# The samples' query attention of a hybrid decoder step: cache loads for two samples at a time, both heads in 1 KB pieces

## The chip, the cores and the metric

One Trainium2 chip; the kernel runs on one of its cores. The time is the device time of one execution in microseconds (us), here the median of three runs. Names used below: TensorE (PE in rows, PEld for its weight loads), VectorE (DVE), ScalarE (ACT), GpSimd (POOL), SyncE (SP). SP computes nothing; it issues the kernel's DMAs in a fixed order, one queue for all of them. DMAs run on 16 DMA engines of the core.

## What is computed

One inference step of a two-layer decoder, for a prompt of 4096 tokens and, beside it, for 8 samples of one new token each. Layer 0 is a dilated sliding-window attention, layer 1 a grouped-query attention over a window of 128 with a learned sink per head: 16 query heads share 2 key-value heads of 64 elements. The change touches layer 1 for the samples only. Cut to that:

```python
def swa_sink_sample(q, kv_ext, n_past, sinks):     # kv_ext: 128 cached rows and the new one
    B, S, HQ, hd = q.shape
    HKV = kv_ext.shape[3]; G = HQ // HKV
    qg = q.reshape(B, S, HKV, G, hd)
    s = jnp.einsum('bskgd,bjkd->bkgsj', qg, kv_ext[:, :, 0]) * hd ** -0.5
...
    p, den = sink_softmax(s, mask, sink)
    o = jnp.einsum('bkgsj,bjkd->bskgd', p, kv_ext[:, :, 1]) / jnp.moveaxis(den, -1, 1)[..., None]
    return o.reshape(B, S, HQ * hd)
```

The cache `cache_b_kv` is laid out as (8 samples, 128 positions, key or value, 2 heads, 64 elements) in float32, so the keys and values of both heads at one position are 256 elements, 1 KB, in one piece of memory, and one head's keys at one position are 256 B.

## The kernel before

The program is unrolled by a Python generator and nothing reorders it afterwards: each engine runs its instructions in the order in which they were written. The prompt is worked in seven passes over 32 tiles of 128 tokens: three passes `a`, then `c`, two passes `b` (pass 4 for key-value head 0, pass 5 for head 1), then `d`. A tile has 48 ticks. In each tick one projection matmul is issued (line 650, `ps_pj<-wt,xT`), and tables (`PB0`, `PB1` for the b passes) say at which tick, counted from the tile's start, the tile's other steps are issued; steps reach into the next two tiles. Of a b tile the steps that matter here are, with the ticks of pass 4 and of pass 5:

- `turn`, -64 and -39: a DMA transpose brings the tile's activations, `xT<-x1s` (L174).
- `load`, -12 and -3: SP loads `tab` (L927), in pass 5 also `KV<-kvd` (L930).
- `kvs`, 37, pass 4 only: SP stores the keys and values of the tile, `kvd<-KV` (L968).
- `tp0` to `tp3`, 93, 94, 100, 103 and 84, 88, 96, 103: four DMA transposes of probabilities, `PT<-PS` (L598), one for each pair of heads. VectorE makes PS.
- `va0` to `va3`, 110, 112, 126, 131 and 96, 109, 124, 127: TensorE multiplies PT by the values, `ps_o<-KV,PT` (through the helper at L97).
- `sum0`, `sum1`: VectorE divides into `uo` (L1033), of which there is one buffer; then `ubd<-uo` (L1050) stores it on SP.

At the end of a tile one copy of a cache to its output goes to SP too (L1596, `out_a_s<-in_cache_a_kv_g`).

The samples' work is a side program, a generator of small steps. `PACE` holds a number for each pass; every `PACE` ticks, in tiles 1 to 29, one step of the side program is taken ("a pump"), and its instructions land between the tiles' own on each engine. `wait()` is four empty steps. In pass 4 the side program runs `samples_kv`, `samples_b(0)` and then the split of pass 5's weights (`weights_pass`, loads at L314); in pass 5 it runs `samples_b(1)` and then pass 6's weights, which begin with a burst of four loads `st<-in_w_o_b`.

`samples_b` (L1312) is what changes. It takes the eight samples in two rounds of four. In each round SP issues four DMAs: for keys, then for values, a load of 127 cached positions (L1334, `s_half<-in_cache_b_kv`), one position to a partition, and a small copy of the new token's row into partition 127 (L1336, `s_half<-kvsd`). Five pumps later TensorE turns the keys (L1341, `ps_kTs`), and scores, softmax and values follow step by step. `s_half` is a pool of four buffers of 128 x 512 float32.

Of the kernel before, what the change touches and what calls it, by code (L numbers as in the profile page):

```python
# [9 lines left out]
F32 = mybir.dt.float32  # L10
# [5 lines left out]
ALU = mybir.AluOpType  # L16
# [36 lines left out]
PD = dict(load=-100, stat=-75, rstd=-67, high=-60, low=-57, turn=-31, loadx=10, gp=42, sq0=47, sq1=57, rstd2=76,  # L53
          add=77, store=85)

PACE = [3.66, 5.6, 5.15, 9, 8.8, 9, 16]
GAP = [0, 0, 0, 0, 0, 0, 0]


# [5 lines left out]
def decoder_kernel(ctx: ExitStack, tc: tile.TileContext, I, O):  # L65
    nc = tc.nc
    dma = nc.sync.dma_start
# [18 lines left out]
    sp = ctx.enter_context(tc.tile_pool(name="samp", bufs=1))  # L86
# [4 lines left out]
    sx_ps = ctx.enter_context(tc.tile_pool(name="sx", bufs=1, space=PSUM))  # L91
# [4 lines left out]
    def mm(out, lhsT, rhs, start, stop):  # L96
        nc.tensor.matmul(out, lhsT, rhs, start=start, stop=stop)  # L97
# [4 lines left out]
    ident = cpool.tile([128, 128], F32, name="ident")  # L102
# [31 lines left out]
    kvsd = dr.tile([NS, 256], F32, name="kvsd")  # L134
# [45 lines left out]
    def s_half():  # L180
        return sp.tile([128, 512], F32, name="s_half", tag="s_half", bufs=4)

    def load_s(src):
        t = s_half()
        n, w = src.shape
        dma(t[:n, :w], src)
        return t[:n, :w]
# [349 lines left out]
    def gate(t, z):  # L537

        nc.scalar.activation(t, z, AF.Tanh, scale=0.5)
        gate2(t, z)  # L540
# [568 lines left out]
    def wait():  # L1109
        for _ in range(WAIT):  # L1110
            yield
# [68 lines left out]
    def s_rope(src, heads):  # L1180

        t1 = sp.tile([128, 512], F32, name="s_rope", tag="s_rope")[:NS]
        t2 = s_half()
        rope_mult(src, rope_s, t1, t2, NS, heads)
        return t1
# [126 lines left out]
    def samples_b(jh, q, z):  # L1312
        snk = sp.tile([NS, 1], F32, name="snk", tag="snk")
        dma(snk, I["sinks_b"][0, jh * 8:(jh + 1) * 8].unsqueeze(1))
        R = s_rope(q[:NS], 8)
        sz = sp.tile([128, 512], F32, name="gate_s", tag="gate_s")
        gate(sz[:NS], z[:NS])
        yield
        yield
        ps = sx_ps.tile([64, 8, NS], F32, name="ps_qTs", tag="sx")  # L1320
        for h in range(8):
            nc.tensor.transpose(ps[:, h, :], R[:, h * 64:(h + 1) * 64], ident[:NS, :NS])
        yield
        QTs = sp.tile([64, NS, 8], F32, name="QTs", tag="QTs")
        nc.vector.tensor_copy(QTs.rearrange("p b h -> p h b"), ps)
        m = sp.tile([8, NS], F32, name="m_s", tag="m_s")
        l = sp.tile([8, NS], F32, name="l_s", tag="l_s")
        on = s_half()
        src = I["cache_b_kv"].rearrange("b j s h e -> j b s h e")
        for q4 in range(2):  # L1330
            bs = slice(4 * q4, 4 * q4 + 4)
            kvt = s_half().rearrange("p (b s e) -> p b s e", b=4, s=2)
            for s in range(2):
                dma(kvt[0:127, :, s, :], src[1:128, bs, s, jh, :])  # L1334
                o = s * 128 + jh * 64
                dma(kvt[127:128, :, s, :], kvsd[bs, o:o + 64].unsqueeze(0))  # L1336
            yield from wait()
            yield
            pk = sx_ps.tile([64, 4, 128], F32, name="ps_kTs", tag="sx")
            for k in range(4):  # L1340
                nc.tensor.transpose(pk[:, k, :], kvt[:, k, 0, :], ident)  # L1341
            yield
            KTs = s_half().rearrange("p (b e) -> p b e", b=4)
            nc.scalar.copy(KTs[:64], pk)
            yield
            yield
            sc = sx_ps.tile([8, 4, 128], F32, name="ps_scs", tag="sx")
            for k in range(4):
                mm(sc[:, k, :], QTs[:, 4 * q4 + k, :], KTs[:64, k, :], True, True)
            yield  # L1350
            nc.vector.tensor_reduce(out=m[:, bs], in_=sc, axis=AX.X, op=ALU.max)
            nc.vector.tensor_scalar(m[:, bs], m[:, bs], SCALE, snk, op0=ALU.mult, op1=ALU.max)
            nc.vector.tensor_scalar(m[:, bs], m[:, bs], -1.0, None, op0=ALU.mult)
            yield
            P = s_half()
            for k in range(4):
                b = 4 * q4 + k
                nc.scalar.activation(P[:8, k * 128:(k + 1) * 128], sc[:, k, :], AF.Exp, bias=m[:, b:b + 1], scale=SCALE,
                                     accum_out=l[:, b:b + 1])
            yield  # L1360
            yield
            ps = sx_ps.tile([128, 4, 8], F32, name="ps_sPb", tag="sx")
            for k in range(4):
                nc.tensor.transpose(ps[:, k, :], P[:8, k * 128:(k + 1) * 128], ident[:8, :8])
            yield
            PTs = sp.tile([128, 4, 8], F32, name="PTsb", tag="PTs")
            nc.vector.tensor_copy(PTs, ps)
            yield
            po = sx_ps.tile([8, 4, 64], F32, name="ps_sob", tag="sx")
            for k in range(4):  # L1370
                mm(po[:, k, :], PTs[:, k, :], kvt[:, k, 1, :], True, True)
            yield
            es = sp.tile([8, 4], F32, name="es_s", tag="es_s")
            nc.vector.tensor_scalar(es, m[:, bs], snk, None, op0=ALU.add)
            nc.scalar.activation(es, es, AF.Exp)
            nc.vector.tensor_tensor(l[:, bs], l[:, bs], es, op=ALU.add)
            nc.vector.reciprocal(l[:, bs], l[:, bs])
            nc.vector.scalar_tensor_tensor(on[:8, q4 * 256:(q4 + 1) * 256].rearrange("p (b e) -> p b e", e=64), po, 0.5,
                                           l[:, bs].unsqueeze(2).to_broadcast([8, 4, 64]), op0=ALU.mult, op1=ALU.mult)
            yield  # L1380
        dma(usd[jh].rearrange("b (h e) -> h b e", e=64), on[:8].rearrange("p (b e) -> p b e", e=64))
        yield from wait()
        o2 = load_s(usd[jh])
        yield from wait()
        nc.vector.tensor_tensor(o2, o2, sz[:NS], op=ALU.mult)
        yield
        dma(ubd_s[:, HV[jh]], o2)
# [147 lines left out]
    def pump(gen, n=1):  # L1535
        for _ in range(n):
            if next(gen, True) is True:
                return

    def side(pi):  # L1540

        if pi < 3:
            if pi == 0:
                yield from s_start()
                samp[0] = yield from weights_pass(0, None, [samp["hS0"]] * 2, False)
            if pi == 2:
                mix_factors()
            yield from samples_a(order[pi][1], *samp[pi])
            yield from ada_units([(v, i) for v in VEC[2 + 2 * pi:4 + 2 * pi] for i in range(2)])
            if pi < 2:  # L1550
                samp[pi + 1] = yield from weights_pass(pi + 1, [G0c] * 2, [samp["hS0"]] * 2)
            else:
                yield from samples_c(3)
        elif pi == 3:
            Gk, G1 = load_cols("Gkv"), load_cols("G1")
            yield from wait()
            samp[4] = yield from weights_pass(4, [Gk, G1, G1], [samp["hSk"], samp["hS1"], samp["hS1"]])
        elif pi == 4:
            yield from samples_kv(samp[4][0])
            yield from samples_b(0, *samp[4][1:])  # L1560
            G1 = load_cols("G1")
            yield from wait()
            samp[5] = yield from weights_pass(5, [G1] * 2, [samp["hS1"]] * 2)
        elif pi == 5:
            yield from samples_b(1, *samp[5])
            yield from samples_d(6)
# [14 lines left out]
    for tick in range(min(at), max(at) + 1):  # L1581
# [6 lines left out]
        pi, it, s = tiles[n][0], n % NB, tick - start[n]  # L1588
        if it == 1 and s == 0:
            begun = tick  # L1590
        if 1 <= it < NB - 2 and (tick - begun) % PACE[pi] >= PACE[pi] - 1:
            pump(sides[pi])
        if n + 1 < N and tick + 1 == start[n + 1]:
            if copies and n >= 2 and order[pi][0] != "c":
                o, i = copies.pop(0)
# [59 lines left out]
```

## Time and profile before

| | us |
|---|---|
| median of 3 runs | 3038.01 |
| lowest and highest run | 3031.45, 3038.73 |
| the profiled execution, its whole time | 3039.8 |
| its span from first to last instruction | 3037.9 |

| engine | busy us | share of the span |
|---|---|---|
| PE | 2898.5 | 95% |
| DVE | 1885.8 | 62% |
| ACT | 1859.2 | 61% |
| POOL | 798.3 | 26% |

Shares are means over seven passes. What a change in the two b passes is worth is read there: pass 4 begins near 1620 us, pass 5 near 2180 us of the span. In the lists of waits a line reads: engine, tile and line that waited, what it waited for, us in total, times, the longest. The chain of work that ended last is followed backwards from the end of the kernel; an engine's name with a q (SPq) is time in which its queue was held by an instruction.

### The profile page before, as it was taken

What the parts mean: (1) busy time and instruction counts of PE and PEld (TensorE: products, weight loads), DVE (VectorE), ACT (ScalarE), POOL (GpSimd) and SP (SyncE); (2) the same over time, 40 slices, a digit from 0 to 9 for tenths busy, and PEclk for the clock granted to TensorE, in tenths of its full rate; (3) what the DMA queues carried; (4) which work ended last, traced back from release to release, by engine and by line L of the source; (5) the groups of instructions that cost most, each with busy time, mean ns of one, the idle gap of its engine ahead of it and who ended that gap; (6) DMA issues with size and microseconds to landing.
All of it is one profiled execution on the core that took longest, in us unless ns stands there. A gap on an engine that the chain in (4) does not pass through costs nothing.

```text
span 3037.9 us, 57543 instructions
## 1 busy us (share of the span) xinstructions
PE 2898.5 (95%) x20600; PEld 1486.8 (49%) x20600; DVE 1885.8 (62%) x4797; ACT 1859.2 (61%) x4606; POOL 798.3 (26%) x989
## 2 busy tenths in 40 slices
PE   7999989999999999998998899999979999999998
PEld 2444434544445444444444566666545555544444
DVE  4655565545556677875665567776756677764443
ACT  4766676555666667766554567666656777763332
POOL 0422111211112333343332223233322222331121
PEclk8999999999999999999999899999999999999999
DMA  7898996787857799779996569777657988798975
GB/s 240 207 250 231 281 260 157 163 184 186 192 128 168 190 235 224 170 174 313 287 257 172 116 136 204 157 147 138 137 115 151 199 190 169 156 223 231 218 200 159
DMA packets 1092888, 585.97 MB, mean 193 GB/s; under 512 B 925156, under 2 KB 1003509, under 8 KB 1089896
## 3 DMA queue, kind: packets, MB, share of 16 engines
q1 hardware_dynamic: 1092600, 582.29, 80.3%
q8 instruction: 161, 2.64, 0.4%
q14 instruction: 127, 1.04, 0.1%
HBM read 243.76 MB, written 159.26 MB: 133 GB/s over the span
## 4 chain that ended last, share of the span: by engine, by line
PE 73%; DMA 8%; DVE 6%; ACT 4%; SPq 4%; issue 3%; POOL 1%; DVEq 0%; POOLq 0%; ACTq 0%
PE ps_pj L650 50%; PE ps_sc L650 7%; PE ps_o L97 4%; DMA PT<-PS 4%; PE ps_sc L97 3%; PE ps_kv L97 3%; SPq L1336 2%; PE ps_sc L562 2%; PE ps_tr L616 1%; PE ps_s L210 1%; PE ps_tr L1000 1%; DMA st<-in_w_in_a_dram 1%; ACT P L584 1%; DMA xT<-usdp 1%; PE ps_ada L210 1%
## 5 line engine op out<-in xcount | busy, mean ns | idle before, releaser
L650 PE MATMUL ps_pj<-wt,xT 128*128 128x512 f16 x9024 | 2180.7, 382 | 33.8 <-ACT ps_pj L631 23.6
L650 PEld LDWEIGHTS <-xT 128*128 128x128 f16 x10368 | 965.4, 98 | 1054.0 <-issue 113.7
L535 POOL TENSOR_TENSOR rope<-rope,rope 128x512 f32<-128x512 f32 x160 | 264.2, 1651 | 899.7 <-DVE rope L530 866.5
L593 DVE SCALAR_TENSOR_TENSOR PS<-P,PS 128x512 f16<-128x512 f32 (+1 forms) x448 | 300.6, 691 | 167.0 <-ACT PS L592 165.9
L530 DVE SCALAR_TENSOR_TENSOR rope<-ps_pj,scl,tab 128x512 f32<-128x512 f32 x320 | 225.0, 744 | 149.7 <-PE ps_pj L650 149.2
L584 ACT ACTIVATE P<-P,nm_b 128x256 f32<-128x256 f32 (+1 forms) x512 | 252.9, 494 | 103.6 <-DVE nm_b L577 102.9
L631 ACT ACTIVATE ps_pj<-bias,scl 128x512 f32<-128x512 f32 x318 | 219.2, 689 | 146.4 <-DVE rope L530 71.1
L650 PE MATMUL ps_sc<-wt,xT 128*128 128x512 f16 x1344 | 297.0, 379 | 0.7 <-DMA xT<-usdp 0.7
L97 PEld LDWEIGHTS <-PT 128*128 128x128 f16 x5076 | 207.3, 98 | 177.6 <-DMA PT<-PS 81.3
L592 ACT ACTIVATE PS<-P 128x512 f16<-128x512 f32 (+1 forms) x448 | 258.0, 597 | 54.9 <-DMA PT<-PS 51.4
L577 DVE CUSTOM_DVE_ANT_0 P<-ps_sc,masks,nsink 128x256 f32<-128x256 f32 (+1 forms) x512 | 249.4, 534 | 4.0 <-PE ps_sc L97 3.9
L577 DVE CUSTOM_DVE_ANT_0 P<-ps_sc,masks,scl 128x256 f32<-128x256 f32 (+1 forms) x384 | 154.4, 450 | 128.0 <-PE ps_sc L562 94.9
L97 PE MATMUL ps_o<-KV,PT 128*128 128x64 f16 x3024 | 131.7, 194 | 46.4 <-DMA PT<-PS 46.4
L97 PE MATMUL ps_sc<-KTb,QTb 128*128 128x256 f16 (+1 forms) x1024 | 153.3, 273 | 10.5 <-ACT QTb L1004 5.3
L584 ACT ACTIVATE P<-P,U 128x256 f32<-128x256 f32 (+1 forms) x256 | 118.3, 463 | 65.1 <-DVE U L577 62.2
L863 DVE TENSOR_TENSOR ss<-ss 128x1 f32<-128x1 f32 x64 | 10.2, 159 | 206.8 <-ACT junk L858 206.5
L97 PEld LDWEIGHTS <-QTb 128*128 128x128 f16 x1024 | 99.2, 98 | 76.0 <-ACT QTb L1004 12.5
L142 POOL TENSOR_SCALAR rm_t<-ss 128x1 f32<-128x1 f32 (+2 forms) x132 | 26.9, 203 | 392.2 <-ACT xs L158 336.2
L1004 ACT COPY QTb<-ps_tr 128x1024 f16<-128x1024 f16 x64 | 64.8, 1012 | 90.4 <-PE ps_tr L1000 90.2
L867 POOL TENSOR_TENSOR rs<-rm_t,mhalf 128x1 f32<-128x1 f32 x64 | 38.9, 607 | 279.2 <-DVE rm_t L866 278.7
L858 ACT ACTIVATE junk<-ps_sc 128x512 bf16<-128x512 f32 x64 | 38.1, 595 | 119.2 <-PE ps_sc L650 114.4
L1045 POOL TENSOR_TENSOR uo<-uo,gate 128x512 f32<-128x512 f32 x64 | 93.1, 1455 | 53.1 <-DVE uo L1033 17.8
(256 smaller groups left out, 3519.6 us busy)
## 6 DMA issues: line engine op xcount, KB each, us to landing
out_a_s_dram<-in_cache_a_kv_g_dram SPq DMA_DIRECT2D x144, 256.0 KB
x_t<-in_x_prompt_dram SPq DMA_DIRECT2D x64, 512.0 KB
st<-in_w_in_a_dram SPq DMA_DIRECT2D x96, 256.0 KB
xsd<-xs SPq DMA_DIRECT2D x32, 512.0 KB
st<-in_ada_w_dram SPq DMA_DIRECT2D x32, 512.0 KB
x1d<-x_t SPq DMA_DIRECT2D x32, 512.0 KB
st<-in_w_in_b_dram SPq DMA_DIRECT2D x32, 512.0 KB
x1s<-xs SPq DMA_DIRECT2D x32, 512.0 KB
```

The lines of the kernel that those rows point to most:

```text
L97: nc.tensor.matmul(out, lhsT, rhs, start=start, stop=stop)
L210: nc.tensor.matmul(ps[q:q + QR, :w.shape[-1]], hS[:, c, :], w, start=c < 4, stop=c + 4 >= nch, tile_position=(0, q))
L530: nc.vector.scalar_tensor_tensor(t[:n, :w].rearrange("p (h e) -> p h e", e=64), s3, scale, tab[:n, o:o + 64].unsqueeze(1).to_broadcast([n, ...
L535: nc.gpsimd.tensor_tensor(a4, a4, b4[:, :, ::-1, :], op=ALU.add)
L577: nc.vector.tensor_tensor_reduce(out=self.P[:, j, :n], in0=self.sc[j][:, :n], in1=self.mask[:, :n], scale=self.nss, scalar=self.init[j], o ...
L584: nc.scalar.activation(self.P[:, j, :n], self.P[:, j, :n], AF.Exp, bias=self.nm[j], scale=-1.0, accum_out=self.l[j])
L592: nc.scalar.activation(S[:, 0], P, AF.Copy, scale=PSC)
L593: nc.vector.scalar_tensor_tensor(S[:, 1], P, PSC, S[:, 0], op0=ALU.mult, op1=ALU.subtract)
L631: nc.scalar.activation(t[f"ps{hf}"], bias[pi, hf], AF.Copy, scale=scl[pi][:, IDS:IDS + 1])
L650: nc.tensor.matmul(t[f"ps{hf}"], t[hT][:, p, c, :], ws()[hf][c][q], start=c == 0 and k == 0 and not biased, stop=c == n - 1 and k == 2, sk ...
L1004: nc.scalar.copy(t["QT"], t["tq"])
L1045: nc.gpsimd.tensor_tensor(t["uo"], t["uo"], t["sz"], op=ALU.mult)
```

## The change

`samples_b` takes four rounds of two samples in place of two rounds of four. A round has one load in place of two: it brings, for two samples, keys and values of both heads, though the call uses one head (`jh`), in pieces of 256 elements (1 KB) in place of 64 (256 B). The buffer keeps its size, 512 elements a partition. The row of the new token is one copy of 512 elements a round in place of two copies of 4 x 64. All steps behind the loads are the same with two samples in place of four, so a call has 32 steps more; `PACE` of passes 4 and 5 goes from 8.8 and 9 to 7.3 ticks.

```diff
-PACE = [3.66, 5.6, 5.15, 9, 8.8, 9, 16]
+PACE = [3.66, 5.6, 5.15, 9, 7.3, 7.3, 16]
...
-        src = I["cache_b_kv"].rearrange("b j s h e -> j b s h e")
-        for q4 in range(2):
-            bs = slice(4 * q4, 4 * q4 + 4)
-            kvt = s_half().rearrange("p (b s e) -> p b s e", b=4, s=2)
-            for s in range(2):
-                dma(kvt[0:127, :, s, :], src[1:128, bs, s, jh, :])
-                o = s * 128 + jh * 64
-                dma(kvt[127:128, :, s, :], kvsd[bs, o:o + 64].unsqueeze(0))
+        src = I["cache_b_kv"].rearrange("b j s h e -> j b (s h e)")
+        for q in range(4):
+            bs = slice(2 * q, 2 * q + 2)
+            kvt = s_half().rearrange("p (b s e) -> p b s e", b=2, e=64)
+            k4 = kvt.rearrange("p b s e -> p b (s e)")
+            dma(k4[0:127], src[1:128, bs])
+            dma(k4[127:128], kvsd[bs].unsqueeze(0))
             yield from wait()
             yield
-            pk = sx_ps.tile([64, 4, 128], F32, name="ps_kTs", tag="sx")
-            for k in range(4):
-                nc.tensor.transpose(pk[:, k, :], kvt[:, k, 0, :], ident)
+            pk = sx_ps.tile([64, 2, 128], F32, name="ps_kTs", tag="sx")
+            for k in range(2):
+                nc.tensor.transpose(pk[:, k, :], kvt[:, k, jh, :], ident)
...
-            for k in range(4):
-                mm(po[:, k, :], PTs[:, k, :], kvt[:, k, 1, :], True, True)
+            for k in range(2):
+                mm(po[:, k, :], PTs[:, k, :], kvt[:, k, 2 + jh, :], True, True)
...
```

How this moves SP's queue is seen at three places. In the rows, 127x4x64 is 127 partitions of four pieces of 64 elements; "x2" stands for two such rows in succession; the changed file is one line shorter, so that L1336 becomes L1335 and L1596 becomes L1595.

SP in pass 4 before, the second round:

```order
L598 DMA_TRANSPOSE PT<-PS 128x8x128 x2
L1596 DMA out_a_s_dram<-in_cache_a_kv_g_dram 16x4096
L1334 DMA s_half<-in_cache_b_kv_dram 127x4x64
L1336 DMA s_half<-kvsd 1x4x64
L1334 DMA s_half<-in_cache_b_kv_dram 127x4x64
L1336 DMA s_half<-kvsd 1x4x64
L1050 DMA ubd_2_276<-uo 128x512
L598 DMA_TRANSPOSE PT<-PS 128x8x128 x2
```

The same pass now, the second round (the fourth stands in the same way) and then the third:

```order
L598 DMA_TRANSPOSE PT<-PS 128x8x128 x2
L1334 DMA s_half<-in_cache_b_kv_dram 127x2x256
L1335 DMA s_half<-kvsd 1x512
L174 DMA_TRANSPOSE xT<-x1s_183 128x16x128
L927 DMA tab<-in_rope_dram 128x128
L968 DMA kvd_245<-KV 128x320
L598 DMA_TRANSPOSE PT<-PS 128x8x128 x2
```

```order
L968 DMA kvd_247<-KV 128x320
L1334 DMA s_half<-in_cache_b_kv_dram 127x2x256
L1335 DMA s_half<-kvsd 1x512
L598 DMA_TRANSPOSE PT<-PS 128x8x128 x2
L1595 DMA out_a_s_dram<-in_cache_a_kv_g_dram 16x4096
L1050 DMA ubd_4_278<-uo 128x512
```

The double load between the two pairs of PT has become single loads that stand, in rounds 2 and 4, between a tile's last PT and the next xT, and in rounds 1 and 3 between the kvd store and the first PT.

SP in pass 5, where the first and the third round stand as the two old rounds did (xT, load, copy, PT); the second and the fourth now:

```order
L598 DMA_TRANSPOSE PT<-PS 128x8x128
L1334 DMA s_half<-in_cache_b_kv_dram 127x2x256
L1335 DMA s_half<-kvsd 1x512
L598 DMA_TRANSPOSE PT<-PS 128x8x128
L174 DMA_TRANSPOSE xT<-x1s_182 128x16x128
```

```order
L598 DMA_TRANSPOSE PT<-PS 128x8x128 x2
L1334 DMA s_half<-in_cache_b_kv_dram 127x2x256
L1335 DMA s_half<-kvsd 1x512
L927 DMA tab<-in_rope_dram 128x128
L930 DMA KV<-kvd_250 128x320
L1050 DMA ubd_6_312<-uo 128x512
L1595 DMA out_a_s_dram<-in_cache_a_kv_g_dram 16x4096
L598 DMA_TRANSPOSE PT<-PS 128x8x128 x2
```

Round 2 has moved between a tile's third and fourth PT, round 4 between its second and third, ahead of four other DMAs.

## Rows read from the trace of the kernel before

**Rows 1.** The page: the chain that ended last, its lines.

```profile
PE ps_pj L650 50%; PE ps_sc L650 7%; PE ps_o L97 4%; DMA PT<-PS 4%; PE ps_sc L97 3%; PE ps_kv L97 3%; SPq L1336 2%; PE ps_sc L562 2%; PE ps_tr L616 1%; PE ps_s L210 1%; PE ps_tr L1000 1%; DMA st<-in_w_in_a_dram 1%; ACT P L584 1%; DMA xT<-usdp 1%; PE ps_ada L210 1%
```

**Rows 2.** PE's timeline: start, us, line, op, tiles, count, [idle before <-releaser].

```profile
1672.35 0.50 PE L97 MATMUL ps_o<-KV,PT 128*128 128x64 f16 x6 [9.02 <-DMA PT<-PS]
...
1736.38 0.82 PE L97 MATMUL ps_o<-KV,PT 128*128 128x64 f16 x12 [10.58 <-DMA PT<-PS]
...
2228.03 0.50 PE L97 MATMUL ps_o<-KV,PT 128*128 128x64 f16 x6 [10.79 <-DMA PT<-PS]
...
2283.11 0.82 PE L97 MATMUL ps_o<-KV,PT 128*128 128x64 f16 x12 [9.45 <-DMA PT<-PS]
```

**Rows 3.** Chain in order of time, 1650 to 1680: start, us, what.

```profile
1654.38 0.42 SPq L1334
...
1654.86 7.71 SPq L1336
...
1669.80 2.50 DMA PT<-PS
```

**Rows 4.** SP's timeline, first load of the other three pairs.

```profile
1715.63 0.43 SPq L1334 DMA_DIRECT2D s_half<-in_cache_b_kv_dram  x1
...
2210.65 0.43 SPq L1334 DMA_DIRECT2D s_half<-in_cache_b_kv_dram  x1
...
2265.13 0.44 SPq L1334 DMA_DIRECT2D s_half<-in_cache_b_kv_dram  x1
```

**Rows 5.** DMA queue, 1657 to 1662: packets, MB, share of 16 engines.

```profile
q1 hardware_dynamic: 355, 0.09, 8.0%
```

**Rows 6.** Stretches: length, busy us (count) by engine, clock, DMA; first four stretches summed.

```profile
sum 16.45, PE 16.45 PEld 8.12 DVE 9.05 ACT 9.69 POOL 2.84; mean PE 4.11 PEld 2.03 DVE 2.26 ACT 2.42 POOL 0.71
...
2386.30:2391.10 4.80, 4.80 (x35) 2.84 (x35) 2.78 (x7) 4.37 (x14) 1.64 (x1) 0.50 0.96 156
1740.00:1760.00 20.00, 20.00 (x174) 12.59 (x171) 13.79 (x40) 12.27 (x32) 5.69 (x5) 1.00 0.57 125
```

**Rows 7.** DMA traffic, 35 to 37 (1 KB pieces), then 2718 to 2719 (4 KB).

```profile
DMA packets 766, 0.74 MB, mean 369 GB/s; under 512 B 46, under 2 KB 766, under 8 KB 766
...
DMA packets 136, 0.45 MB, mean 448 GB/s; under 512 B 27, under 2 KB 27, under 8 KB 136
```

**Rows 8.** A calm tile of pass 4: SP's timeline, then PE's.

```profile
1746.42 2.64 SPq L598 DMA_TRANSPOSE PT<-PS  x2
...
1758.06 0.32 SPq L968 DMA_DIRECT2D kvd<-KV  x1
...
1748.75 0.51 PE L97 MATMUL ps_o<-KV,PT 128*128 128x64 f16 x12
...
1766.95 0.51 PE L97 MATMUL ps_o<-KV,PT 128*128 128x64 f16 x12
```

**Rows 9.** The first tile of pass 4: SP's timeline, then PE's.

```profile
1647.80 0.34 SPq L968 DMA_DIRECT2D kvd<-KV  x1
...
1655.69 0.34 PE L97 MATMUL ps_o<-KV,PT 128*128 128x64 f16 x6
```

**Rows 10.** A calm tile of pass 5: SP's timeline, then PE's.

```profile
2311.43 2.92 SPq L598 DMA_TRANSPOSE PT<-PS  x2
...
2315.53 0.38 SPq L1050 DMA_DIRECT2D ubd<-uo  x1
...
2317.01 2.65 SPq L598 DMA_TRANSPOSE PT<-PS  x2
...
2325.11 0.51 PE L97 MATMUL ps_o<-KV,PT 128*128 128x64 f16 x12
...
2326.10 0.51 PE L97 MATMUL ps_o<-KV,PT 128*128 128x64 f16 x12
```

**Rows 11.** Waits, 2376 to 2392; then the chain from 2376 to 2387.

```profile
PE ps_sc L97 <- DVE nm_b L577: 4.4, 1, 4.4
...
2376.13 8.55 DMA ubd<-uo
```

More of the change, by code (lines that the diff above doesn't have):

```diff
@@ L1328, in samples_b @@
         on = s_half()
-        src = I["cache_b_kv"].rearrange("b j s h e -> j b s h e")
-        for q4 in range(2):
-            bs = slice(4 * q4, 4 * q4 + 4)
-            kvt = s_half().rearrange("p (b s e) -> p b s e", b=4, s=2)
-            for s in range(2):
-                dma(kvt[0:127, :, s, :], src[1:128, bs, s, jh, :])
-                o = s * 128 + jh * 64
-                dma(kvt[127:128, :, s, :], kvsd[bs, o:o + 64].unsqueeze(0))
+        src = I["cache_b_kv"].rearrange("b j s h e -> j b (s h e)")
[5 more added lines that the diff above has]
+            dma(k4[127:128], kvsd[bs].unsqueeze(0))
             yield from wait()
             yield
-            pk = sx_ps.tile([64, 4, 128], F32, name="ps_kTs", tag="sx")
-            for k in range(4):
-                nc.tensor.transpose(pk[:, k, :], kvt[:, k, 0, :], ident)
+            pk = sx_ps.tile([64, 2, 128], F32, name="ps_kTs", tag="sx")
+            for k in range(2):
+                nc.tensor.transpose(pk[:, k, :], kvt[:, k, jh, :], ident)
             yield
-            KTs = s_half().rearrange("p (b e) -> p b e", b=4)
+            KTs = s_half().rearrange("p (b e) -> p b e", b=4)[:, 0:2]
             nc.scalar.copy(KTs[:64], pk)
@@ L1346, in samples_b @@
             yield
-            sc = sx_ps.tile([8, 4, 128], F32, name="ps_scs", tag="sx")
-            for k in range(4):
-                mm(sc[:, k, :], QTs[:, 4 * q4 + k, :], KTs[:64, k, :], True, True)
+            sc = sx_ps.tile([8, 2, 128], F32, name="ps_scs", tag="sx")
+            for k in range(2):
+                mm(sc[:, k, :], QTs[:, 2 * q + k, :], KTs[:64, k, :], True, True)
             yield
@@ L1355, in samples_b @@
             P = s_half()
-            for k in range(4):
-                b = 4 * q4 + k
+            for k in range(2):
+                b = 2 * q + k
                 nc.scalar.activation(P[:8, k * 128:(k + 1) * 128], sc[:, k, :], AF.Exp, bias=m[:, b:b + 1], scale=SCALE,
@@ L1361, in samples_b @@
             yield
-            ps = sx_ps.tile([128, 4, 8], F32, name="ps_sPb", tag="sx")
-            for k in range(4):
+            ps = sx_ps.tile([128, 2, 8], F32, name="ps_sPb", tag="sx")
+            for k in range(2):
                 nc.tensor.transpose(ps[:, k, :], P[:8, k * 128:(k + 1) * 128], ident[:8, :8])
             yield
-            PTs = sp.tile([128, 4, 8], F32, name="PTsb", tag="PTs")
+            PTs = sp.tile([128, 2, 8], F32, name="PTsb", tag="PTs")
             nc.vector.tensor_copy(PTs, ps)
             yield
-            po = sx_ps.tile([8, 4, 64], F32, name="ps_sob", tag="sx")
-            for k in range(4):
-                mm(po[:, k, :], PTs[:, k, :], kvt[:, k, 1, :], True, True)
+            po = sx_ps.tile([8, 2, 64], F32, name="ps_sob", tag="sx")
+            for k in range(2):
+                mm(po[:, k, :], PTs[:, k, :], kvt[:, k, 2 + jh, :], True, True)
             yield
-            es = sp.tile([8, 4], F32, name="es_s", tag="es_s")
+            es = sp.tile([8, 2], F32, name="es_s", tag="es_s")
             nc.vector.tensor_scalar(es, m[:, bs], snk, None, op0=ALU.add)
@@ L1377, in samples_b @@
             nc.vector.reciprocal(l[:, bs], l[:, bs])
-            nc.vector.scalar_tensor_tensor(on[:8, q4 * 256:(q4 + 1) * 256].rearrange("p (b e) -> p b e", e=64), po, 0.5,
-                                           l[:, bs].unsqueeze(2).to_broadcast([8, 4, 64]), op0=ALU.mult, op1=ALU.mult)
+            nc.vector.scalar_tensor_tensor(on[:8, q * 128:(q + 1) * 128].rearrange("p (b e) -> p b e", e=64), po, 0.5,
+                                           l[:, bs].unsqueeze(2).to_broadcast([8, 2, 64]), op0=ALU.mult, op1=ALU.mult)
             yield
```

## The prediction

> **What bounds the kernel now.** The chain of waits comes first [rows 1]: TensorE's matmul groups make most of it, and one line of SP's queue, L1336, has 2%, some 60 us. A DMA issue that holds its queue is rare, so I read what it does to TensorE. In TensorE's timeline over the two b passes, four waits for a transposed probability tile PT stand out: 9.02, 10.58, 10.79 and 9.45, together 39.8 us [rows 2]. The chain around the first says why [rows 3]: SP issues the cache load L1334 in 0.42 us, the tiny L1336 behind it then takes 7.71 us, the pair comes once more, and only then the transpose PT, whose result takes 2.50 us and starts TensorE. The other three pairs look alike [rows 4].
>
> Why is L1336 slow? While it stands, the whole core moves 355 packets in 5 us, 8.0% of sixteen engines [rows 5]: one engine, 14.1 ns for a piece of 256 B, 18 GB/s. The load has 127 rows of four pieces: 508 x 14.1 = 7.2 us. So it runs on one engine, and SP is held until nearly all of its pieces are taken.
>
> From the first load's issue (T) to TensorE's restart are 17.97 us (1654.38 to 1672.35), 17.4 (2210.65 to 2228.03), 18.0 (2265.13 to 2283.11), and 20.75 in the second place, where a store stood ahead of PT [rows 2 to 4]. Two drains are 14.3 us, so the rest (start of the load, PT itself) is 3.1 to 3.7, once 6.4. I use restart = T + drain + 3.4.
>
> Behind the four waits TensorE works at half clock (granted 0.50, the 1.2 GHz level): 1672.35 to 1677.80, 1736.40 to 1739.20, 2228.05 to 2230.70 and 2283.15 to 2288.70, together 16.45 us [rows 6]; half of that, 8.2 us, is lost. **The four places cost 39.8 + 8.2 = 48 us now,** the most that can be won.
>
> **The change part by part.** *The load.* Still 127 rows and eight loads, but each takes two samples with both heads: 254 pieces of 1 KB, 260 KB where it was 130 KB. Pieces halve, bytes double, half of them never used. What one engine makes of 1 KB pieces alone, this trace does not show. The nearest row is 1 KB pieces on all sixteen: 369 GB/s, 23.1 per engine, 44.4 ns a piece [rows 7], so 11.3 us a load. Bounds: the fastest stretch, with 4 KB pieces, 448 GB/s or 28 per engine [rows 7], gives 9.3 us; 18 GB/s as now gives 14.3. I take 11.0, close to the row with the same piece and a little under, since this engine has the memory to itself. A load thus drains in 11.0 in place of 7.2 us, all eight in 88 in place of 58.
>
> A rule speaks against the change too. The Trainium skill, page "DMA: Bandwidth & Descriptors", section "Why a DMA increments its semaphore by 16 and not by 1", says that 127 partitions put a whole transfer on one engine, and its section "Specifications" gives one engine about 27 GiB/s. By that figure a load would drain in an estimated 9.0 us, and the sum below would come to about 3031.
>
> *The pairs come apart.* Eight single blocks in place of four double ones: TensorE restarts at T + 11.0 + 3.4 = T + 14.4, in place of T + 18. I assume that PT waits for the drain even where SP is let go before its end, since PT's share on that engine queues behind the load. What a block costs depends on how long TensorE can work on from T without PT. The order of the changed kernel tells what stands behind each load, calm tiles tell when TensorE wants it:
> - Pass 4, loads 1 and 3 stand between the kvd store and the first two PTs. At load 1 the store ends 1648.14 and the first values start 1655.69, 7.5 us [rows 9]; in a calm tile 1758.38 and 1766.95, 8.6 [rows 8]. Waits 6.9 and 5.8.
> - Pass 4, loads 2 and 4 stand behind a tile's last PT. From there to the next values are 1749.06 to 1766.95, 17.9 us [rows 8], 3.5 more than 14.4, in which xT, tab and kvd must be issued: no wait. But the keys must land for TensorE's own transposes, five pumps later: 36.5 ticks of 48, in a tile of 18.2 us (1748.75 to 1766.95) [rows 8], 13.9 us. Load 4 is issued nearly on its tick: 1.5 us; load 2 well before it: 0.
> - Pass 5, loads 1 and 3 stand where the old pairs stood. From T, TensorE worked 6.6 us (2210.65 to 2228.03 less 10.79) and 8.5 (2265.13 to 2283.11 less 9.45) [rows 2, 4]. Waits 7.8 and 5.9.
> - Pass 5, load 2 stands between the third and the fourth PT: 2318.3 (half of the 2.65 us for two) to the last values 2326.10, 7.8 us [rows 10]. Wait 6.6.
> - Pass 5, load 4 stands behind the second PT, ahead of tab, KV, the ubd store and two PTs. For PT alone: 2314.35 to 2325.11, 10.8 us [rows 10], wait 3.6. But a late ubd store has a price of its own: VectorE cannot write uo before it has landed. Once TensorE waited 4.4 us for that: the store took 8.55 us, to 2384.68 [rows 11], and TensorE restarted 1.6 us later [rows 6], having stopped 5.8 us after the store's issue. Calm, it is issued at 2315.53 [rows 10], 1.2 us behind T; put behind the load it lands near T + 14. Wait 6.5.
>
> Sum: 6.9 + 5.8 + 1.5 + 7.8 + 5.9 + 6.6 + 6.5 = 41.0 us against 39.8: **+1.2 us.** The drain's bounds (9.3 and 14.3) move six waits by 1.7 less or 3.3 more each: -10 or +20.
>
> *The clock.* Four long waits become six of 6 to 8 us. The 4.4 us wait was followed by 4.80 us at half clock, no less than the long ones with a mean of 4.11 [rows 6]. Six times that, halved, is 12 to 14; I take 13.4 against 8.2: **+5.2 us.** Below zero this term goes only with fewer waits.
>
> *The pace.* 29 tiles are 1392 ticks: at 8.8 and 9 they give 158 and 154 pumps, at 7.3 they give 190; the code needs 32 more. So the side work ends about where it did, and the burst of four weight loads that made the store of the 4.4 us wait late keeps its place behind the second PT. TensorE's matmuls and transposes are as many as before. VectorE gets 32 instructions more, ScalarE 8, all of half the size; at VectorE's mean in a calm stretch, 13.79 us for 40 [rows 6], they are at most 11 us of its time. They hide: in that stretch TensorE is full and VectorE idle for 6.2 of 20 us. With no cover they would cost those 11 us; I take 0.
>
> **The rivals.**
> *A 1 KB load drains as fast as the old one* (7.2 us). For it: half as many pieces, and short pieces move fewer bytes a second in every row. Against: 36 GB/s on one engine, where the fastest row has 28 [rows 7]. Restart T + 10.6: waits 3.1, 2.0, 4.0, 2.1, 2.8 and 2.7, sum 16.7; whether such short ones lower the clock no row shows, so 0 to 13 us more, middle 6.6. 48 - 23.3 = 25 us faster: 3013. The Trainium skill, page "DMA: Bandwidth & Descriptors", section "Specifications", would have it so: pieces under 512 B are read, modified and written, so below line rate. The measured step from 18 to 23 GB/s is far from double.
> *SP is held by the number of pieces, or the load spreads over engines* (3.6 us): restart T + 7, no wait left: 48 us faster, 2990. No row supports it.
> *Late keys* (slower): TensorE's in-order transposes of the keys, ps_kTs, at loads 2 and 4 of pass 4, which I hold calm. It decides from a landing later than T + 13.9. At a drain of 12 us, load 4 waits 2.5 and load 2 some 1, both with 2.2 of half clock behind them, and the other six waits grow by 1 each: 12.4 less the 1.5 counted, 3055. At 13 us it is 3064.
> *The code does not do as it says* is excluded: the order of the changed kernel has single 127x2x256 loads.
>
> **How the numbers follow.** The profiled execution took 3039.8 us, 1.8 above the median of the runs, 3038.0. +1.2 + 5.2 = +6.4 gives 3046.2 on it and **3044** on the median. Same means within 0.3%, about what a measurement of this kernel can tell: 9 us, 3029 to 3047. Chances: forecast 0.58 (own range 3034 to 3054: 0.39 same, 0.17 slower, 0.02 faster); as fast as the old 0.17; no block 0.05; late keys 0.17 (slower); the rest, side work shifting by some us, 0.03 (same). Faster 0.24, same 0.42, slower 0.34. The range takes in the rival at 3013 and late keys to a drain of some 12.4 us: 3011 to 3058; outside lie the 2990 case and half of the late keys.
>
> **What would show it.** L1335 (L1336 before) holding SP some 8 to 10 us in eight places, packets at 23 GB/s meanwhile, six waits of TensorE of 6 to 8 us and none for PT at loads 2 and 4 of pass 4, six stretches at 0.50. Wrong if L1335 takes 4 us (the drain is not by bytes), if PT returns well before the load's end (no queueing on that engine), or if ps_kTs waits more than 2 us.

## The result and the profile after

The changed kernel took **3062.1 us** (median of six runs, 3054.3 to 3064.7) beside 3036.8 for the kernel before: ratio 1.0087, 95% interval 1.0076 to 1.0099, some 26 us slower. The prediction was 3044, within 0.3%, range 3011 to 3058: wrong, and the time lies above its range. The mechanism that it described is there; two of its terms were too small.

The page of after, the line that answers to [rows 1]: the line that held SP is still in the chain, with half its share.

```profile
PE ps_pj L650 49%; PE ps_sc L650 7%; DMA PT<-PS 4%; PE ps_o L97 4%; PE ps_sc L97 3%; PE ps_kv L97 2%; PE ps_sc L562 2%; SPq L1335 1%; PE ps_tr L616 1%; ACT P L584 1%; DMA st<-in_w_in_a_dram 1%; PE ps_s L210 1%; PE ps_tr L1000 1%; DVE P L577 1%; PE ps_ada L210 1%
```

PE's timeline of after, one row for each of the eight loads, four of pass 4 and four of pass 5 [rows 2]; the bracket is the wait and what ended it.

```profile
1656.80 0.50 PE L97 MATMUL ps_o<-KV,PT 128*128 128x64 f16 x6 [6.13 <-DMA PT<-PS]
...
1709.07 0.38 PE L1340 MATMUL ps_kTs<-ident,s_half 128*64 128x128 f32 x2 [1.59 <-DMA s_half<-kvsd]
...
1755.32 0.82 PE L97 MATMUL ps_o<-KV,PT 128*128 128x64 f16 x12 [6.72 <-DMA PT<-PS]
...
1807.67 0.38 PE L1340 MATMUL ps_kTs<-ident,s_half 128*64 128x128 f32 x2 [3.16 <-DMA s_half<-kvsd]
...
2225.48 0.50 PE L97 MATMUL ps_o<-KV,PT 128*128 128x64 f16 x6 [7.10 <-DMA PT<-PS]
...
2273.22 0.82 PE L97 MATMUL ps_o<-KV,PT 128*128 128x64 f16 x12 [7.53 <-DMA PT<-PS]
...
2315.01 0.82 PE L97 MATMUL ps_o<-KV,PT 128*128 128x64 f16 x12 [5.81 <-DMA PT<-PS]
...
2362.08 1.01 PE L97 MATMUL ps_sc<-KTb,QTb 128*128 128x256 f16 x4 [6.95 <-DVE nm_b L577]
```

The list of TensorE's waits over both b passes of after (tile and line that waited, releaser, us in total, times, longest):

```profile
PE ps_o L97 <- DMA PT<-PS: 37.5, 13, 7.5
PE ps_sc L97 <- DVE nm_b L577: 10.3, 3, 6.9
PE ps_sc L97 <- ACT QTb L1004: 9.8, 9, 1.8
PE ps_kTs L1340 <- DMA s_half<-kvsd: 4.8, 2, 3.2
```

At the eight places TensorE now waits 45.0 us, where it waited 39.8 at four. The same list of before has 45.1 for PT, 5.1 for nm_b, 5.3 for QTb and nothing for the keys.

SP's timeline of after around the fourth and the third load of pass 4, then the second load's own row [rows 3, 4]. The copy behind the load holds SP for 7.4 and 7.7 us. The transposes behind that then take 5 us to issue: 5.32 for a pair of PT, where a calm pair takes 2.64 [rows 8], and 5.06 for one xT, where a calm one takes some 2.5.

```profile
1791.34 2.64 SPq L598 DMA_TRANSPOSE PT<-PS  x2
1794.04 0.43 SPq L1334 DMA_DIRECT2D s_half<-in_cache_b_kv_dram  x1
1794.52 7.67 SPq L1335 DMA_DIRECT2D s_half<-kvsd  x1
1802.30 5.06 SPq L174 DMA_TRANSPOSE xT<-x1s  x1
...
1740.97 0.28 SPq L1334 DMA_DIRECT2D s_half<-in_cache_b_kv_dram  x1
1741.31 7.39 SPq L1335 DMA_DIRECT2D s_half<-kvsd  x1
1748.81 5.32 SPq L598 DMA_TRANSPOSE PT<-PS  x2
...
1695.35 0.43 SPq L1334 DMA_DIRECT2D s_half<-in_cache_b_kv_dram  x1
```

The DMA traffic while that third load drains alone, 1744 to 1748 [rows 5]: 92 pieces of 1 KB in 4 us are 43.5 ns each, on about one of sixteen engines.

```profile
DMA packets 92, 0.09 MB, mean 24 GB/s; under 512 B 0, under 2 KB 92, under 8 KB 92
...
q1 hardware_dynamic: 92, 0.09, 6.8%
```

TensorE's stretches at half clock in the two passes: first the sum of before's five, then of after's nine, and of these the stretch behind the late keys and one that no load explains (columns as in [rows 6]; 0.50 is the granted clock, the 1.2 GHz level).

```profile
sum 21.65, PE 21.64 PEld 11.20 DVE 12.00 ACT 14.24 POOL 4.48; mean PE 4.33 PEld 2.24 DVE 2.40 ACT 2.85 POOL 0.90
...
sum 35.89, PE 35.89 PEld 19.82 DVE 18.52 ACT 21.93 POOL 3.70; mean PE 3.99 PEld 2.20 DVE 2.06 ACT 2.44 POOL 0.41
...
1808.71:1812.13 3.42, 3.42 (x13) 1.70 (x12) 0.00 (x0) 0.00 (x0) 0.00 (x0) 0.50 0.84 132
...
2634.74:2638.15 3.41, 3.41 (x13) 1.84 (x14) 2.59 (x10) 2.33 (x7) 0.00 (x0) 0.50 0.86 161
```

**Where the time went.** I measure both passes from the first copy into QTb of pass 4 to the last of pass 5. Each kernel has two profiled executions, the second from the last two runs below. The sum rows give the length and PE's busy time: before, before again, after, after again.

```profile
sum 1051.26, PE 995.92 PEld 595.39 DVE 720.97 ACT 710.68 POOL 306.61; mean PE 497.96 PEld 297.70 DVE 360.48 ACT 355.34 POOL 153.30
...
sum 1045.28, PE 992.91 PEld 593.40 DVE 721.37 ACT 710.11 POOL 306.40; mean PE 496.46 PEld 296.70 DVE 360.68 ACT 355.06 POOL 153.20
...
sum 1070.63, PE 1007.38 PEld 597.04 DVE 728.66 ACT 712.38 POOL 309.67; mean PE 503.69 PEld 298.52 DVE 364.33 ACT 356.19 POOL 154.84
...
sum 1072.87, PE 1005.15 PEld 596.03 DVE 730.27 ACT 711.86 POOL 308.89; mean PE 502.58 PEld 298.02 DVE 365.13 ACT 355.93 POOL 154.44
```

Length less PE's busy time is idle time; half of the half-clock stretches is lost to the clock (21.65 and 15.0 us of stretches before, 35.9 and 31.3 after); what is left is TensorE's work at full clock.

| us, both b passes | before, twice | after, twice | difference of means | predicted |
|---|---|---|---|---|
| length | 1051.3, 1045.3 | 1070.6, 1072.9 | +23.5 | +6.4 |
| TensorE idle at the loads | 39.8, 39.0 | 45.0, 46.8 | +6.5 | +1.2 |
| lost to the half clock | 10.8, 7.5 | 17.9, 15.7 | +7.6 | +5.2 |
| TensorE idle elsewhere | 15.5, 13.4 | 18.2, 21.0 | +5.2 | 0 |
| TensorE's work at full clock | 985.1, 985.4 | 989.4, 989.5 | +4.2 | 0 |

The passes are 23.5 us longer, where the ratios of the runs say 24 to 26. (Ahead of pass 4, where nothing was changed, after's two traces are 4.8 and 5.8 us shorter than before's, so these four executions as a whole differ by only 14.6 and 21.8 us; the ten traces of this document scatter by 8 us there.) The last two rows of the table, 9.4 us, lie away from the eight loads.

### The profile page after: what moved, and what is told of

It reads as the page before. It is cut to its first block, busy times and chain, and to the rows that moved or that the text cites. A ratio compares the mean times of both kernels' runs of the same rounds, so it can differ in the third digit from the quotient of the medians.

```text
span 3052.5 us, 57610 instructions
## 1 busy us (share of the span) xinstructions
PE 2909.8 (95%) x20600; PEld 1488.6 (49%) x20600; DVE 1891.4 (62%) x4829; ACT 1861.1 (61%) x4614; POOL 803.3 (26%) x989
## 3 DMA queue, kind: packets, MB, share of 16 engines
q8 instruction: 161, 2.64, 0.4%
## 4 chain that ended last, share of the span: by engine, by line
PE 71%; DMA 10%; DVE 6%; ACT 5%; SPq 3%; issue 3%; POOL 1%; DVEq 0%; POOLq 0%; ACTq 0%
PE ps_pj L650 49%; PE ps_sc L650 7%; DMA PT<-PS 4%; PE ps_o L97 4%; PE ps_sc L97 3%; PE ps_kv L97 2%; PE ps_sc L562 2%; SPq L1335 1%; PE ps_tr L616 1%; ACT P L584 1%; DMA st<-in_w_in_a_dram 1%; PE ps_s L210 1%; PE ps_tr L1000 1%; DVE P L577 1%; PE ps_ada L210 1%
## 5 line engine op out<-in xcount | busy, mean ns | idle before, releaser
L97 PE MATMUL ps_kv<-wt,xT 128*128 128x256 f16 x768 | 106.5, 276 | 0.0
```

## Experiments

Two theories stood at the start. **A:** a load of 127 partitions drains on one engine and holds SP and the transposes behind it; that makes the waits and the half clock, and the closer pace of the side program costs little. **R:** the loads cost about what they did, and the pace, or the doubled number of small steps, makes the difference.

**The pace alone.** The kernel before, with only this:

```diff
-PACE = [3.66, 5.6, 5.15, 9, 8.8, 9, 16]
+PACE = [3.66, 5.6, 5.15, 9, 7.3, 7.3, 16]
```

> The kernel before with nothing changed but PACE 7.3 in passes 4 and 5. Theory A (the change costs through eight drains on one engine: TensorE's waits behind them and the half clock behind the waits; pace is a few us): 0 to 5 us over before, four waits of 9 to 11 us for PT as before, perhaps at other places in a tile. Rival R (the denser side program costs most of the 25 us): 15 to 25 us over before.

Measured: 3043.2 us beside 3032.7, ratio 1.0036 (1.0022 to 1.0050), +11 us. It lies between the theories: less than R, more than the 5 us that A allowed.

**The load undone, the rest of the change kept.** Rounds of two samples at the new pace, but each round loads its own head in two loads of 254 pieces of 256 B (the steps behind go back to the old indices):

```diff
...
-            k4 = kvt.rearrange("p b s e -> p b (s e)")
-            dma(k4[0:127], src[1:128, bs])
-            dma(k4[127:128], kvsd[bs].unsqueeze(0))
+            for s in range(2):
+                dma(kvt[0:127, :, s, :], src[1:128, bs, s, jh, :])
+                o = s * 128 + jh * 64
+                dma(kvt[127:128, :, s, :], kvsd[bs, o:o + 64].unsqueeze(0))
...
```

> The changed kernel (two samples a round, pace 7.3), but each round loads only its own head: keys and values apart, twice 254 pieces of 256 B in place of 254 of 1 KB. A: the two loads drain in 254 x 14.1 x 2 = 7.2 us in place of 11, so TensorE restarts at T + 10.6 to 11 in place of T + 14.3: six waits of 2 to 4 us, sum 15 to 20 in place of 45, at most half of the half-clock stretches; 20 to 35 us under the changed kernel, 0 to 12 under before. R: as the changed kernel, within 5 us. If SP is held by the number of pieces alone (508 against 254), it is slower than the changed kernel.

Measured: 3023.4 us, ratio to before 0.9968 (0.9955 to 0.9980): 9 us faster than before and some 36 faster than the change, at the far end of what A gave. SP's timeline of this kernel at its first round shows two drains with half as many pieces as before: 254 x 14.1 ns = 3.6 us each, and SP held for 3.1. The row under it is from its list of waits: TensorE waits 17.6 us for PT over both passes, where the change has 37.5.

```profile
1649.81 0.28 SPq L1334 DMA_DIRECT2D s_half<-in_cache_b_kv_dram  x1
1650.20 3.15 SPq L1336 DMA_DIRECT2D s_half<-kvsd  x1
1653.39 0.41 SPq L1334 DMA_DIRECT2D s_half<-in_cache_b_kv_dram  x1
1653.85 3.08 SPq L1336 DMA_DIRECT2D s_half<-kvsd  x1
...
PE ps_o L97 <- DMA PT<-PS: 17.6, 13, 3.7
```

A round thus drains for 7.2 us when it brings its own head alone, and for 11 with the other head in 1 KB pieces; whether the bytes or the width of the pieces make that, this run doesn't separate. Two samples at a time are no harm but a gain: this kernel has the pace of the experiment before it and is 20 us faster (0.9968 and 1.0036). Eight blocks of 7 us cost less than four of 14; the wide pieces give that away.

**The block taken away, in the kernel before.** Each load is split into 112 partitions and 15:

```diff
-                dma(kvt[0:127, :, s, :], src[1:128, bs, s, jh, :])
+                dma(kvt[0:112, :, s, :], src[1:113, bs, s, jh, :])
+                dma(kvt[112:127, :, s, :], src[113:128, bs, s, jh, :])
```

> The kernel before, with each cache load cut in two, 112 partitions and 15 partitions, in place of one of 127; rounds of four samples, 256 B pieces and pace as before. A: 112 rows go over sixteen engines and 15 over fifteen, some 28 to 32 pieces an engine, the small copy is held under 1 us, SP loses only the four more issues of a round (1.7 us): no wait of TensorE for PT over 2 us in the places of the four, 35 to 48 us under before. R: within 5 us of before.

Measured: **2985.4 us**, ratio 0.9842 (0.9829 to 0.9856), 48 us faster than before: the whole price that the prediction gave to the four blocks. This version beats both kernels. SP's timeline at its first round: nothing is held, the same two loads pass in 4 us.

```profile
1652.63 0.57 SPq L1334 DMA_DIRECT2D s_half<-in_cache_b_kv_dram  x1
1653.26 0.93 SPq L1335 DMA_DIRECT2D s_half<-in_cache_b_kv_dram  x1
1654.24 0.71 SPq L1337 DMA_DIRECT2D s_half<-kvsd  x1
1654.99 0.43 SPq L1334 DMA_DIRECT2D s_half<-in_cache_b_kv_dram  x1
...
1656.01 0.61 SPq L1337 DMA_DIRECT2D s_half<-kvsd  x1
1657.08 1.33 SPq L598 DMA_TRANSPOSE PT<-PS  x1
```

The sum row of its two passes leaves 998.77 - 984.98 = 13.8 us of idle, and PE's 985.0 us are the work at full clock found above: no half clock is left (the granted clock is 1.00 in both passes).

```profile
sum 998.77, PE 984.98 PEld 591.42 DVE 721.51 ACT 710.14 POOL 307.12; mean PE 492.49 PEld 295.71 DVE 360.75 ACT 355.07 POOL 153.56
```

**The block taken away, in the changed kernel.**

```diff
-            dma(k4[0:127], src[1:128, bs])
+            dma(k4[0:112], src[1:113, bs])
+            dma(k4[112:127], src[113:128, bs])
```

> The changed kernel, with each cache load cut into 112 and 15 partitions; two samples, both heads, 1 KB pieces and pace 7.3 as changed. A: the drain falls from 11 us to about 1, no block is left: 55 to 70 us under the changed kernel, and above e3 by what pace and the smaller steps cost, 0 to 8 us. R: 0 to 10 us under the changed kernel.

Measured: 2994.9 us, ratio 0.9878 (0.9864 to 0.9891). Against the change at 1.0087 that is 2.1%, 63 us by the ratios: the price of the eight blocks, where the four had 48. And with no block left, the change still costs 10.9 us over the version above (0.9878 less 0.9842), more than the 0 to 8 that A allowed. So A holds for the blocks, but not for the rest. That rest can be the pace, the small steps or the doubled bytes; the next two runs tell.

**Pace alone, with no blocks.** The split kernel before, with the pace of both passes, then of pass 5 only:

```diff
-PACE = [3.66, 5.6, 5.15, 9, 8.8, 9, 16]
+PACE = [3.66, 5.6, 5.15, 9, 7.3, 7.3, 16]
```

> The kernel before with its loads split over 112 and 15 partitions (so no block of SP is left, 2985 us) and, beside that, only the pace of passes 4 and 5 at 7.3 ticks. Theory P (the closer pace costs by itself: the side program's instructions stand closer together, TensorE gets short waits in pass 5 with half clock behind them): 8 to 12 us over the split kernel before, 2993 to 2998, the same as the split changed kernel. Theory S (the pace cost 11 us in the first experiment only because it put the blocks in other places, and what divides the two split kernels are the smaller steps): within 3 us of 2985.

```diff
-PACE = [3.66, 5.6, 5.15, 9, 8.8, 9, 16]
+PACE = [3.66, 5.6, 5.15, 9, 8.8, 7.3, 16]
```

> As the run before it, but the pace of pass 4 stays at 8.8 and only pass 5 goes from 9 to 7.3 ticks. Theory P, by the traces of the first runs, puts nearly all of the pace's cost into pass 5 (pass 4 grew by 1 to 2 us, pass 5 by 6 to 10): 6 to 10 us over the split kernel before, 2991 to 2995. If the cost is spread evenly over both passes: 4 to 6. Theory S: within 3.

Measured: 2995.4 us, ratio 0.9875 (0.9856 to 0.9893), and 2989.2, ratio 0.9850 (0.9832 to 0.9869). The first is the split changed kernel to within its interval, so the pace alone is enough for the 10 us, and small steps or doubled bytes need add nothing; the difference of two such ratios is good to some 7 us. Pass 5 alone accounts for 2 to 4 of it by ratio and median, where I had expected nearly all of it from single traces, in which it had 6 to 10. With the same 7 us to either side, how the cost divides over the passes stays open.

By the traces the pace's cost has three parts. Beside the split kernel before, the split one with both paces is 13.4 us longer in the two passes: 7.5 of idle time of TensorE, 3.6 lost to half clock and 2.3 of work at full clock. Beside the mean of the two traces of before, the pace with the blocks in place has 3.3, 5.0 and 1.7. Each is one trace of its kernel.

How the waits arise is seen in the second of the split kernels. Its list of waits in the two passes has TensorE wait 9.1 us for QTb, where the split kernel before (second row) has 5.6:

```profile
PE ps_sc L97 <- ACT QTb L1004: 9.1, 11, 2.0
...
PE ps_sc L97 <- ACT QTb L1004: 5.6, 5, 2.0
```

From the first copy into QTb to the last, the seven traces with 7.3 ticks in pass 5 have 8.8 to 10.6, the three with 9 ticks 5.3. What stands in front of QTb is seen at the wait of 2.00 us. TensorE has its transposes ps_tr done at 2440.24 and stops at 2441.67 (its timeline; L1000 feeds QTb):

```profile
2439.63 0.61 PE L1000 MATMUL ps_tr<-identh,Q 128*128 128x128 f16 x8
...
2443.66 0.50 PE L97 MATMUL ps_sc<-KTb,QTb 128*128 128x256 f16 x3 [2.00 <-ACT QTb L1004]
```

VectorE's timeline ahead of that, then ScalarE's:

```profile
2433.49 0.69 DVE L219 TENSOR_TENSOR s_half<-s_half 64x512 f32<-64x512 f32 x1
2434.21 1.64 DVE L220 TENSOR_TENSOR s_half<-s_half 9x512 f32<-9x512 f32 x1
2435.94 1.47 DVE L593 SCALAR_TENSOR_TENSOR PS<-P,PS 128x512 f16<-128x512 f32 x1
2437.33 0.53 DVE L577 CUSTOM_DVE_ANT_0 P<-ps_sc,masks,nsink 128x256 f32<-128x256 f32 x1
...
2437.91 0.51 ACT L584 ACTIVATE P<-P,nm_b 128x256 f32<-128x256 f32 x1 [3.20 <-DVE nm_b L577]
...
2441.16 0.71 ACT L288 ACTIVATE wt<-st,scl 128x512 f16<-128x512 f32 x1
...
2442.59 1.02 ACT L1004 COPY QTb<-ps_tr 128x1024 f16<-128x1024 f16 x1
```

Two additions of the side program (L219, L220) stand on VectorE ahead of the maxima nm_b, so ScalarE waits 3.20 us for them before its exponentials, and a weight of the side program (L288) stands on ScalarE ahead of QTb. Each engine takes them in the order in which they were written. A pump every 7.3 ticks in place of 9 puts the same steps closer together: the sixteen weights of line 288 in pass 5 start within 99 us of each other here, within 123 in the split kernel before. This is one wait, read from one trace; that the others arise in the same way isn't shown.

The order of SP has its share too. In the split kernel with both paces the four weight loads `st<-in_w_o_b` stand between the third PT and the fourth, and TensorE waits 5.11 us for the latter (SP's timeline, then PE's):

```profile
2301.11 2.13 SPq L314 DMA_DIRECT2D st<-in_w_o_b_dram  x4
2303.35 4.19 SPq L598 DMA_TRANSPOSE PT<-PS  x1
...
2313.39 0.82 PE L97 MATMUL ps_o<-KV,PT 128*128 128x64 f16 x12 [5.11 <-DMA PT<-PS]
```

The split kernel before lost 2.7 us to the same loads behind the second PT, the changed kernel 3.1 there. In pass 4 of the same split kernel TensorE waits once for 2.07 us for VectorE's `w_acc` (L255), a step of the side program too, and in the split kernel before not at all. So the two split kernels at 7.3 ticks agree in their totals, but not in every wait that makes them.

**Both kernels once more,** for a second profile of each.

> The changed kernel as it is, for a second profiled execution. The first was its fastest of six, and its two b passes were 19 us longer than before while the medians differ by 25. If the remaining 6 us lie in these passes, a second trace shows them there as more waits or half clock (25 us in all, the eight waits at the loads 45 to 48); if they are scatter between executions, passes 4 and 5 come out again 17 to 21 us longer and the rest of the span makes the difference.

> The kernel before as it is, for a second profiled execution beside the one above. Passes 4 and 5 should come out within 2 us of the first trace (565 and 486); stretches of identical code outside of them show how far one execution differs from another.

Measured: 3058.1 us, ratio 1.0080 (1.0064 to 1.0096), and 3033.4, ratio 0.9999 (0.9986 to 1.0011). The passes differ by 27.6 us in these two traces, by 19.4 in the first two. For before, pass 5 came out 5 us shorter than in its first trace, not within 2: one trace of 1050 us of this work is good to some 3 us to either side, which is why the table has two of each.

## Why the prediction was wrong

**The block: right.** SP is held behind all eight loads, on a single engine, and only then comes PT. Even after SP is let go the transposes are late: at six places they are slow to issue, at the other two (the first load of each pass) they issue in 2.7 and 2.5 us, but TensorE restarts only 5.9 us after the issue began. Splitting the load removes all of it in both kernels. The 48 us that the prediction put on the four places is what the split gave. The Trainium skill, page "DMA: Bandwidth & Descriptors", section "Why a DMA increments its semaphore by 16 and not by 1", says that the count of engines, at most 16, divides the slowest dimension, so that 127 gives one; the traces agree, with 92 pieces in 4 us at 6.8% of sixteen engines, and no copy held for a microsecond behind the split load.

**The drain: right.** I took 11.0 us for 254 pieces (43.3 ns each), close to the 44.4 ns of [rows 7]; the trace has 43.5. At the five places where PT ends the wait, TensorE restarts 13.8 to 14.6 us after T, where I had 14.4. SP was held 7.3 to 7.7 us (up to 8.3 in the second execution), not 8 to 10: it is let go earlier, and the rest of the drain is found in the slow transposes, as I had assumed for PT. The rival in which a 1 KB load drains as fast as the old is refuted: the 1 KB pieces gave 24 GB/s on the engine where 256 B gave 18.

**The six waits for PT or the ubd store: right.** Predicted 6.9, 5.8, 7.8, 6.6, 5.9 and 6.5, sum 39.5; measured 6.13, 6.72, 7.10, 7.53, 5.81 and 6.95, sum 40.2 (the second execution 42.2). The clock behind these six: 25.7 us at half clock (24.5), so 12.8 lost where I took 13.4. The fourth load of pass 5 went by the route named, over the ubd store: VectorE could not write uo. But its 6.5 came out by luck. By the figures beside it TensorE stops 5.8 us after the store's issue, so at T + 7.0, and restarts 1.6 us after T + 14: that is 8.6. In the trace the landing and the restart are as I had them (VectorE writes uo from T + 14.4, TensorE restarts at T + 15.9), but TensorE had stopped only at T + 8.9.

**The late keys: the first step that failed.** For loads 2 and 4 of pass 4 I held that only keys that land later than T + 13.9 cost anything, and put 0 and 1.5 us. The keys came at T + 13.7 and T + 13.6, and yet TensorE waited 1.59 and 3.16 (the second execution 1.57 and 2.98), the latter over the 2 us that I had named as a sign of being wrong: it had reached them at T + 12.1 and T + 10.5. Two things made that time shorter.

First, 13.9 is 36.5 ticks at a tile's mean length (13.8 by the figures given), and the ticks are not equally long. A tick has one matmul of line 650; counted by these, the 36 or 37 ticks ahead of the keys took some 12 us at load 2 and 13 at load 4. Second, the five pumps run from the pump's tick, not from the issue. By the same count TensorE stood at load 4's tick between 1791.5 and 1791.9; SP issued the load only at 1794.04, since two PTs stood ahead of it until 1793.98 (timeline above), so it left some 2.3 us behind its tick, where I had taken it as issued "nearly on its tick". Load 2 did leave on its tick, and had lost its time to the short ticks alone.

With the stretch at half clock behind it the term is 4.8 + 1.7 = 6.5 us where I had 1.5. The late-keys rival named the place, but tied it to a drain of 12 us; it came at 11. (Its terms make 12.4 after the 1.5 is taken off, so 3056 and not 3055.)

**The pace: the step that cost most.** I took 0 and measured 10 us: +10.5 with the blocks in place and +10 without, and the split changed kernel stands 10.9 above the split one of before. The step weighed the 40 short instructions by their busy time, against TensorE's full stretch as cover, and bounded them by 11 us. But the pace moves every step of the side program closer to the next, the split of the weights too, and these cost by their place in an in-order queue. In the wait shown, 2.3 us on VectorE ahead of the maxima and 0.7 on ScalarE ahead of QTb stand before a wait of 2.0 us, while both engines are idle a third of the time or more [rows 6]. Behind some of these short waits TensorE is at half clock as well: the last of after's nine stretches (2634.74) stands behind a wait of 1.52 us for QTb. The 40 instructions themselves, which the step priced, are absent from the runs with the pace alone, and the cost was the same. Having bounded the term by 11 us, I should have carried that end into the range; 3044 + 11 and 5 for the late keys would have reached 3060.

**Sum.** Undoing the eight blocks gives 63 us. In the two traces of the changed kernel the waits at the loads are 46 us and half of the stretches behind them 14, together 60, where I had 41.0 + 13.4 = 54.4; most of the difference is the late keys, 5 us. The pace adds 10. Beside the 48 us of the four blocks before, that is 63 + 10 - 48 = +25 us in place of +6.4.

**Open.** TensorE's own work at full clock grew by 4.2 us in the changed kernel, with as many matmuls of the prompt as before. The pace alone gives 2 of it, and some 3 are left when the eight blocks are gone; what makes the rest I haven't shown.

## What to carry to other kernels

A DMA issue that takes microseconds in an in-order queue points at the load ahead of it: ask how many engines that load runs on, and split an odd count of partitions (127 into 112 and 15) before working on the size of its pieces. Wider pieces only pay when their bytes are wanted: on one engine four times the bytes in a piece took three times the time. And a closer pace of background steps isn't free where an engine is idle a third of the time; look at what would stand directly ahead of the results that the busy engine waits for.

## What the runs showed that was not expected

SP is not held for the whole drain. At the third load it came free at 1748.70, 7.7 us after T; the traffic from there to 1754 still has 633 - 514 = 119 pieces of 512 B to 2 KB, those of the load, nearly half of its 254:

```profile
DMA packets 634, 0.25 MB, mean 48 GB/s; under 512 B 514, under 2 KB 633, under 8 KB 634
```

Part of the price is thus found in the transposes behind the load, and SP's share in the chain fell from 2% to 1% while the time rose. What lets SP go at that point the runs don't tell.

A short wait can have a clock price as large as its own: waits of 0.85 and 1.52 us, 2 us apart, end in the stretch of 3.41 us at 0.50 from 2634.74, 1.7 us lost. It doesn't have to: in the second execution of the same kernel the same two waits, 0.76 and 1.52 us, are followed by none. PE's timeline of the first:

```profile
2632.18 0.52 PE L97 MATMUL ps_o<-KV,PT 128*128 128x64 f16 x12 [0.85 <-DMA PT<-PS]
...
2634.66 0.99 PE L97 MATMUL ps_sc<-KTb,QTb 128*128 128x256 f16 x4 [1.52 <-ACT QTb L1004]
```
